# One pair of output products moved ahead of the transposes in each attention chunk, and one gate product at the Fourier head tied behind another

## The chip, the core and the metric

The kernel runs on one core of a Trainium2 chip. The core's engines run side by side, each through its own queue in order: TensorE (PE in the profile, its weight loads as PEld), VectorE (DVE), ScalarE (ACT), GpSimd (POOL) and SyncE (SP), which here issues DMAs only. The metric is the device time of one execution in microseconds, and of several runs the median.

## The reference

Two layers are applied to 2048 prompt tokens and, on its own, to 512 sample tokens, all of width 1024 in float32:

```python
def attention_layer(x, g, w_in, w_out, sink, rel_bias):
    h = rmsnorm(x, g);  z = h @ w_in            # q, k, v and gate
    o = banded_gqa_with_sink(q, k, v, rel_bias, sink)   # |i-j| <= 128, 16 heads of 64, 4 kv heads
    return x + (o * jax.nn.silu(gate)) @ w_out
def fourier_layer(x, g, w_gate, w_out):
    h = rmsnorm(x, g)
    f = jnp.fft.fftn(hg, axes=(1, 3), norm="ortho").real   # hg: h in 4 groups of 256 channels
    return x + (f * jax.nn.silu(h @ w_gate)) @ w_out
```

A last rmsnorm follows. Attention is computed in blocks of 128 queries, each with its own block of keys and the two beside it, a bias from a table and a sink per head.

## The kernel before, in words

Every product of float32 matrices is made of three matmuls on a high and a low part of each factor (high by high, high by low, low by high), summed in PSUM.

**Attention phase.** The tokens are taken in five chunks of 512 (`CHUNKS`): the sample's first, then the prompt's four; here they are the first to the fifth or last chunk. After its projections of k and v, a chunk runs a loop of 19 steps (`for n in range(19)`, about line 1188). The 8 head pairs by 2 pairs of query blocks make 16 rounds, and step n works on up to four rounds at once. The order within a step is written out in the table `PERIOD` (`FIRST` for the first chunk). The entries that matter here, in the table's order, with the engine:

- S1, S2 (PE): the scores of two query blocks, each six matmuls into `spt`, two half arrays side by side (`scores`, line 661).
- b1b, b1a, b2a, b2b (DVE): bias and row minimum of the scores of one block and one head (`biased`, line 680). e1b, e1a and so on (ACT): their exponentials.
- m2a, m1b, m1a: the division by the row's sum, on DVE (line 703) or ACT (701).
- T0, T1 (PE): 12 transposes of the divided weights of a block (line 720) into `tp`; hi0, hi1 (ACT, 733) and lo0, lo1 (DVE, 737) take their high and low parts to `pts`.
- AV1, AV2 (PE, 780): weights by values; add (DVE, 810), mul (POOL): the gated output.
- A and B (PE): the slots for products that don't depend on this step's attention.

On PE, and for these operations on DVE and ACT, the written order is kept by a chain of ordering ties (`chain`, `seq`, `pe`). What stands in A and B comes from `fills(n)`. Each entry is a pair of half products: one runs on the upper 64 rows of the array, the other on the lower 64, at the same time, three matmuls each (`beside`, line 512). Up to step 14 they are projections, at steps 15 and 16 products of the chunk's output projection (weights `wo`, input `uT`). At step 15 `t3` lies in the PSUM bank `pj_72` and `t2` in `pj_73`. When a product goes on in the other row half of its bank, `swapped` (line 528) first puts an empty PE instruction there that waits until the last matmul of the first half is finished:

```python
if before:
    wait = pe(PE.nop())
    for ins in before:
        tc.add_manual_dep(wait.ins, ins.ins.name, DONE, reason="other rows of a bank")
```

`beside` calls it once, for all the pairs that it is given, before the first of them. At step 15 the transposes T1 belong to the last head pair; those of its two other blocks follow at step 16, as that step's T0 and T1.

**Fourier phase.** It works through ten pairs of 128-token tiles (the first: tiles 16 and 17 of the sample). Here the order on each engine is set by the scheduler of the framework, from the order of the code and the dependencies. `gates(pr, hooks)` computes the gates of a pair in four sums W, Z, X and again W, with the weights B11, T1, T2, B22, T3, N4 and, for X, four tiles `b21` (b in the profile) that SP loads one by one: each step of X asks for the next tile (`more`, line 1463). `prod(ps, left, right, ks, first, ...)` issues a product, and takes as a last argument an instruction behind which it is ordered. In the same stretch PE computes the transforms `z17`, `z19` and so on (line 1425) into double banks that are shared with the transposes `trb`; ACT and DVE take these away (lines 1364, 1371, 1377, 1378). x1_4 and x1_0 are the inputs of a later pair; SP loads them (line 1321) when their places are free.

Of the kernel before, what the change touches and what calls it, by code (L numbers as in the profile page):

```python
# [55 lines left out]
def encoder(  # L56
# [147 lines left out]
    def attention_phase():  # L204

        with ExitStack() as es:
# [307 lines left out]
            def beside(*pairs):  # L514

                swapped([(unit[0].last, h) for pair in pairs for h, unit in enumerate(pair) if unit is not None])
                for upper, lower in pairs:
                    both = []
                    for h, unit in enumerate((upper, lower)):
                        if unit is not None:  # L520
                            both.append((unit[0], h) + unit[0].parts(unit[1], slice(64 * h, 64 * h + 64)))
                    for i, j in ((0, 0), (0, 1), (1, 0)):
                        for out, h, a, b in both:
                            out.last[h] = pe(PE.matmul(out.ps, a[i], b[j], **out.flags()))  # L524
# [567 lines left out]
            for c in range(len(CHUNKS)):  # L1092
# [41 lines left out]
                four = range(4)  # L1134

                def fills(n):

                    t0, t1, t2, t3 = op_tiles
                    if n < 15:
                        x, y = (o + (t3,))[n + 1 : n + 3]  # L1140
                        return [((x, 4 + k), (y, k)) for k in four], [((y, k), (x, 4 + k)) for k in four]
                    if n == 15:
                        return [((t3, 4 + k), (t2, k)) for k in range(2)], [((t2, k), (t3, 4 + k)) for k in range(2)]
                    if n == 16:
                        return [((t2, 2 + k), (t1, k)) for k in four], [((t1, k), (t2, 2 + k)) for k in four]
                    return [], []
# [43 lines left out]
                for n in range(19):  # L1190
                    if c == 0:
                        if n + 5 < len(fetches):
                            fetches[n + 5]()
                    if n % 2 == 0 and n < 14:
                        at[n // 2 + 1].start(None if c else last_fetch[0])
                    if c and n < 16:
                        loads[n + 4]()
                    chain.setdefault(PE, None)
                    first, second = fills(n)
                    if n == 16:  # L1200
                        beside(*first[:1])
                        first = first[1:]
                    order = [a for a in (PERIOD if c else FIRST) if n < 15 or a[0] not in ("hi0", "lo0")]
                    if n == 1 and c:
                        order.sort(key=lambda a: a[0] == "qL")
                    if n >= 15:
                        for name, behind in (("hi0", ("T0",)), ("lo0", ("m2a", "m2b"))):
                            at_ = max(i for i, a in enumerate(order) if a[0] in behind)
                            order.insert(at_ + 1, (name, 1))
                    for name, back in order:  # L1210
                        m = n - back
                        if name == "A":
                            beside(*first)
                        elif name == "B":
                            beside(*second)
                        elif name == "qH":
                            if c and 0 <= m < 15:
                                high_q.append(evacs[m + 1])
                            if high_q:
                                low_q.append(high_q.pop()())  # L1220
                        elif name == "sc":
                            if 0 <= m < 15:
                                high_q.append(evacs[m + 1]())
                        elif name == "W":
                            for i in (n + 4,) if n < 15 else (19,) if n == 16 else ():
                                low_w.append(highs[i]())
                        elif name == "WL":
                            if low_w:
                                low_w.pop()()
                        elif name == "side":  # L1230
                            side(n)
                        elif name == "qL":
                            if low_q:
                                low_q.pop()()
                            if k_lows:
                                k_lows.pop()()
                        elif name[:5] == "extra":
                            if n < 17:
                                for i in range(4 * n + 2 * int(name[5]), 4 * n + 2 * int(name[5]) + 2):
                                    extra(i)  # L1240
                        elif 0 <= m < 16 and (name, m) != ("AV2", 15):
                            at[m // 2].ops[2 * (m % 2)][name]()
                    if n % 2 and n < 15:
                        at[n // 2 + 1].sinks()
# [11 lines left out]
    def fourier_phase(tail):  # L1256
        with ExitStack() as es:
# [189 lines left out]
            def prod(out, a, b, ks, first, behind=None):  # L1447

                for k in ks:
                    cs = slice(k * P, (k + 1) * P)  # L1450
                    end = matmul3(
                        out, (a[0][:, cs], a[1][:, cs]), b[k], first and k == 0, k == 3, not first, None if k > ks[0] else behind
                    )
                return end

            b21 = []
# [9 lines left out]
            def gates(pr, hooks):  # L1466

                n, A, S = pr.n, pr.A, pr.S
                W = psum2.tile([P, 512], F32, tag="acc", name=f"W{n}")
                Z = psum2.tile([P, 512], F32, tag="acc", name=f"Z{n}")  # L1470
                X = psum2.tile([P, 512], F32, tag="acc", name=f"X{n}")

                def x_step(k):
                    prod(X, A[0, 1], b21[4 * n : 4 * n + 4], (k,), True)
                    more()

                def silu(c, i, half):
                    th = main.tile([P, 512], F32, tag="xr", bufs=3, name=f"gt{pr.ts[i]}_{half}")
                    ACT.activation(th, c, AF.Silu)
                    t = pr.ts[i]  # L1480
                    dst, t0 = (s2d[0], t) if t < SEQ // P else (s2d[1], t - SEQ // P)
                    POOL.dma_start(dst[t0 * P : (t0 + 1) * P, half * 512 : half * 512 + 512], th)

                def hook(i):
                    for h in hooks.get(i, ()):
                        h()

                four = range(4)
                c = xtile([P, 2, 512], F32, f"c{n}")
                c11, c22 = c[:, 0], c[:, 1]  # L1490
                prod(W, A[0, 0], wg["B11"], four, True)
                ACT.copy(c11, W)
                hook(0)
                x_step(0)
                if pr is pairs[-1]:

                    more()
                    more()
                prod(Z, S[1], wg["T1"], four, True)
                ACT.copy(c22, Z)  # L1500
                hook(1)
                prod(W, S[2], wg["T2"], four, False)
                c12 = fp.tile([P, 512], F32, tag="c12", bufs=1, name=f"c12_{n}")
                ACT.copy(c12, W)
                hook(2)
                x_step(1)
                prod(Z, S[4], wg["B22"], four, False)
                DVE.tensor_tensor(c12, c12, Z, ALU.add)
                silu(c12, 0, 1)
                hook(3)  # L1510
                x_step(2)
                prod(W, S[3], wg["T3"], four, False)
                last_c[0] = DVE.tensor_tensor(c22, c22, W, ALU.add)
                silu(c22, 1, 1)
                hook(4)
                x_step(3)
                DVE.tensor_tensor(c11, c11, X, ALU.add)
                silu(c11, 0, 0)
                if pr is not pairs[-1]:
                    hook(5)  # L1520
                prod(W, A[1, 1], wg["N4"], (0, 1), False)
                if pr is pairs[-1]:
                    hook(5)
                prod(W, A[1, 1], wg["N4"], (2, 3), False)
                silu(W, 1, 0)
                hook(6)

            wg = {w: [None] * 4 for w in ("B11", "T1", "T2", "B22", "T3", "N4")}
# [40 lines left out]
            for i, s in enumerate(tail):  # L1569
# [7 lines left out]
                if 1 <= i < 9:  # L1577
                    w, k = split_steps[i - 1]
# [523 lines left out]
            A, S = ALU.add, ALU.subtract  # L2102
# [241 lines left out]
```

## Time and profile before

| | before |
|---|---|
| median of the timed runs | 1534.37 us (1533.88, 1534.37, 1534.41) |
| the profiled execution | 1535.48 us, span 1533.7 us |
| granted TensorE clock, mean | 0.998 |
| PE busy | 1520.7 us, 99% of the span |
| DVE, ACT, POOL busy | 73%, 58%, 30% of the span |
| matmuls of `pj` from `wo`, `uT` | 360, mean 390 ns |
| data moved by DMA | 372.71 MB, mean 243 GB/s |

Step 15 of the five chunks lies at about 164.6, 373.0, 577.8, 783.2 and 979.9 us (start of A); the stretch of the Fourier head that the change touches is from 1031 to 1058 us.

In a timeline row stand the start, the duration from the first start to the last end, engine, line, operation, result and inputs, the count, and in brackets the idle time of the engine before it and whose end ended it. Rows of like instructions that follow each other are put together. PE rows of `x12` overlap each other: matmuls on the two row halves run at the same time, and the next starts before the last has ended. A row of waits gives the total, the number and the longest. In a DMA row stand the count, the size and the median time from issue to landing.

### The profile page before, as it was taken

To read this page: it belongs to the slowest core of one execution; us is meant where nothing else is said; L and a number is where in the kernel's file an instruction comes from. 1 tells how busy PE (TensorE), PEld (TensorE's weight loads), DVE (VectorE), ACT (ScalarE), POOL (GpSimd) and SP (SyncE) were. 2 spreads that over 40 slices of the span, in tenths; PEclk is the share of its full clock that TensorE was granted. 3 is DMA by queue.
4 is the path that set the end of the run, shared out by engine and by line. 5 is a ranking of instruction groups with operands and counts; after the bars stand their busy time and mean duration, and the time that the engine had idled before them with its cause. 6 is when DMAs were issued, how large, how long until landed. Compare 5 with 4: busy or idle time off the path is not lost.

```text
span 1533.7 us, 33665 instructions
## 1 busy us (share of the span) xinstructions
PE 1520.7 (99%) x13150; PEld 1351.5 (88%) x13150; DVE 1119.0 (73%) x2431; ACT 890.3 (58%) x1925; POOL 453.1 (30%) x616
## 2 busy tenths in 40 slices
PE   9999999999999999999999999999999999999998
PEld 7999889999899998999988899888888888888886
DVE  5898665777538775468764577667888878888896
ACT  6788534787237883268862577646655654243343
POOL 2576652422414323315124142222212111011100
PEclk9999999999999999999999999999999999999999
DMA  8687687785857766867649666584667679557852
GB/s 310 230 308 250 231 337 279 218 304 172 317 202 239 248 215 239 300 212 228 226 169 380 226 211 234 208 298 165 238 207 250 210 247 413 169 180 277 298 184 91
DMA packets 100730, 372.71 MB, mean 243 GB/s; under 512 B 11235, under 2 KB 22251, under 8 KB 83420
## 3 DMA queue, kind: packets, MB, share of 16 engines
q1 hardware_dynamic: 82716, 297.38, 56.1%
q0 software_dynamic: 16688, 70.04, 11.8%
q10 hardware_dynamic: 1168, 3.15, 0.6%
q8 instruction: 103, 1.69, 0.4%
q14 instruction: 55, 0.45, 0.1%
HBM read 280.06 MB, written 90.47 MB: 242 GB/s over the span
## 4 chain that ended last, share of the span: by engine, by line
PE 88%; DVE 7%; issue 2%; ACT 2%; DMA 1%; POOL 0%; POOLq 0%; DVEq 0%; SPq 0%; ACTq 0%
PE pj L524 27%; PE W L134 6%; PE pj L134 6%; PE av L780 6%; PE tp L134 5%; PE spt L661 5%; PE av L134 5%; PE spt L134 4%; PE tp L720 3%; PE Wo L134 3%; PE Z L134 3%; PE fo L134 2%; PE z L1425 2%; PE Zo L134 2%; PE X L134 2%
## 5 line engine op out<-in xcount | busy, mean ns | idle before, releaser
L524 PE MATMUL pj<-h,wg 64*128 64x512 f32 x1920 | 437.7, 388 | 0.0
L524 PE MATMUL pj<-h,wq 64*128 64x512 f32 x1560 | 379.0, 389 | 0.0
L524 PEld LDWEIGHTS pj<-h,wg 64*128 64x128 f32 x1920 | 332.1, 184 | 13.1
L524 PEld LDWEIGHTS pj<-h,wq 64*128 64x128 f32 x1560 | 284.4, 184 | 9.3 <-DVE q L580 0.2
L680 DVE CUSTOM_DVE_ANT_0 S<-spt,b 128x385 f32<-128x385 f32 (+1 forms) x320 | 164.8, 524 | 80.0 <-PE spt L661 77.2
L688 ACT ACTIVATE S<-S 128x385 f32<-128x385 f32 (+1 forms) x320 | 189.2, 592 | 54.9 <-DVE S L680 35.5
L733 ACT CAST pts<-tp 128x768 fp32r<-128x768 f32 (+1 forms) x160 | 121.3, 758 | 77.3 <-PE av L780 43.0
L737 DVE TENSOR_TENSOR pts<-tp,pts 128x768 fp32r<-128x768 f32 (+1 forms) x160 | 144.0, 900 | 11.9 <-ACT pts L733 11.4
L825 POOL TENSOR_TENSOR uT<-o,uT 128x256 fp32r<-128x256 f32 x75 | 56.4, 752 | 228.2 <-ACT uT L821 227.9
L780 PE MATMUL av<-pts,v 64*128 64x256 f32 (+3 forms) x1680 | 122.2, 262 | 1.0 <-DVE pts L737 0.9
L661 PE MATMUL spt<-kwin,qab 64*128 64x384 f32 (+1 forms) x960 | 121.9, 340 | 0.9 <-DVE S L680 0.7
L134 PE MATMUL fo<-wo,tTu 128*128 128x512 f32 x480 | 113.7, 392 | 0.0
L780 PEld LDWEIGHTS av<-pts,v 64*128 64x128 f32 (+1 forms) x1680 | 108.3, 159 | 3.4 <-DVE pts L737 1.6
L134 PEld LDWEIGHTS fo<-wo,tTu 128*128 128x128 f32 x480 | 88.7, 188 | 18.0
L720 PEld LDWEIGHTS tp<-ident,S 64*128 64x128 f32 x1792 | 90.4, 138 | 8.0 <-DVE pts L737 2.6
L720 PE MATMUL tp<-ident,S 64*128 64x64 f32 x1792 | 93.3, 223 | 0.1
L816 POOL TENSOR_TENSOR o<-o,s 128x256 f32<-128x256 f32 x75 | 55.7, 743 | 109.6 <-DVE o L810 86.2
L661 PEld LDWEIGHTS spt<-kwin,qab 64*128 64x128 f32 x960 | 83.7, 187 | 3.7 <-issue 1.8
L703 DVE TENSOR_SCALAR S<-S 128x384 f32<-128x384 f32 (+1 forms) x192 | 84.4, 468 | 0.3
L279 DVE SCALAR_TENSOR_TENSOR h<-xk,g0s,h 128x512 fp32r<-128x512 f32 x40 | 46.9, 1185 | 51.1 <-ACT h L278 51.1
L524 PE MATMUL pj<-wo,uT 64*128 64x512 f32 x360 | 74.7, 390 | 0.0
L278 ACT ACTIVATE h<-xk,g0s 128x512 fp32r<-128x512 f32 x40 | 28.7, 724 | 77.1 <-POOL xk L274 76.3
(379 smaller groups left out, 3360.2 us busy)
## 6 DMA issues: line engine op xcount, KB each, us to landing
wo<-wsd SPq DMA_DIRECT2D x32, 1024.0 KB, 6.4
wq<-wsd SPq DMA_DIRECT2D x31, 1024.0 KB, 6.6
wg<-wsd SPq DMA_DIRECT2D x31, 1024.0 KB, 5.9
x<-x1d SPq DMA_DIRECT2D x40, 512.0 KB, 4.0
b<-b21d SPq DMA_DIRECT2D x40, 512.0 KB, 5.1
b<-rowd SPq DMA_DIRECT2D x40, 384.0 KB, 4.1
xs<-in_x_dram SPq DMA_DIRECT2D x23, 512.0 KB, 6.1
s2d<-gt POOLq DMA_DIRECT2D x40, 256.0 KB, 4.0
```

The lines of the kernel that those rows point to most:

```text
L134: ins = pe(PE.matmul(out, a[i], b[j], start=start and i + j == 0, stop=stop and i == 1, skip_group_check=more))
L524: out.last[h] = pe(PE.matmul(out.ps, a[i], b[j], **out.flags()))
L661: pe(PE.matmul(spt[j][:, 2 + k0 * P : 2 + k1 * P], res["q"][rows, qp, b * P : (b + 1) * P], kwin[g][rows, kp, b * P + k0 * P : b * P + k1 ...
L680: seq(DVE, DVE.tensor_tensor_reduce(out=s[:, e0:e1], in0=ps[:, 1 + e0 : 1 + e1], in1=st["bias"][:, j, 386 - e1 : 386 - e0][:, ::-1], scale ...
L688: last_exp[0] = seq(ACT, ACT.activation(s[:, e0:e1], s[:, e0:e1], AF.Exp, bias=s[:, 386:387], scale=-1.0, accum_out=s[:, 387:388]))
L703: seq(DVE, DVE.tensor_scalar(s[:, ks], s[:, ks], den, None, ALU.mult))
L720: pe(PE.transpose(ps[h][:, kb, j, :], s[rows, j, 1 + kb * P : 1 + (kb + 1) * P], ident[rows, rows]))
L733: seq(ACT, ACT.copy(hi, ps))
L737: seq(DVE, DVE.tensor_tensor(lo, ps, f32(hi), ALU.subtract))
L780: last[i][h] = pe(PE.matmul(to, v, pt, start=not swap and n == 0, stop=swap and n == len(todo[h]) - 1, skip_group_check=True,))
L816: eng.tensor_tensor(o, o, s, ALU.mult)
L825: low = eng.tensor_tensor(lo, o, f32(hi), ALU.subtract)
```

## The change

At step 15 the slot A gets three pairs instead of two, the third in a `beside` of its own, and B one instead of two. At the first Fourier pair (`n` is 0) the product of W with T2 is ordered behind the end of X's first step.

```diff
                     if n == 15:
-                        return [((t3, 4 + k), (t2, k)) for k in range(2)], [((t2, k), (t3, 4 + k)) for k in range(2)]
+                        return [((t3, 4), (t2, 0)), ((t3, 5), (t2, 1)), ((t2, 0), (t3, 4))], [((t2, 1), (t3, 5))]
...
                         if name == "A":
-                            beside(*first)
+                            beside(*first[:2] if n == 15 else first)
+                            if n == 15:
+                                beside(*first[2:])
...
                 def x_step(k):
-                    prod(X, A[0, 1], b21[4 * n : 4 * n + 4], (k,), True)
+                    x_end = prod(X, A[0, 1], b21[4 * n : 4 * n + 4], (k,), True)
                     more()
+                    return x_end
...
-                x_step(0)
+                x_end = x_step(0)
...
-                prod(W, S[2], wg["T2"], four, False)
+                prod(W, S[2], wg["T2"], four, False, None if n else x_end)
```

On PE in the fourth chunk, the order around step 15's T1 (`tp<-ident,S_7_1`) and S2 (`spt<-kwin`):

```order
 L524 MATMUL pj_72<-wo_0_4_8482,uT_5_7577 128x512
 L524 MATMUL pj_73<-wo_0_0_8188,uT_1_6454 128x512
+L524 MATMUL pj_73<-wo_0_0_8188,uT_0_6407 128x512
+L524 MATMUL pj_72<-wo_0_4_8482,uT_4_7273 128x512
+L524 MATMUL pj_73<-wo_0_0_8188,uT_0_6407 128x512
+L524 MATMUL pj_72<-wo_0_4_8482,uT_4_7273 128x512
+L524 MATMUL pj_73<-wo_0_0_8188,uT_0_6407 128x512
+L524 MATMUL pj_72<-wo_0_4_8482,uT_4_7273 128x512
 L720 MATMUL tp<-ident,S_7_1_8616 128x64 x12
 L661 MATMUL spt_74<-kwin,qab_7_8351 128x384
```

The six matmuls with `uT_0` and `uT_4` stood behind S2's six matmuls, as the first pair of B, and stand ahead of T1 now. The empty instruction with the wait stands ahead of the first of them, in both orders. In the other chunks the rows are the same but for the numbers.

On PE at the Fourier head, before:

```order
L134 MATMUL W_15122<-wB_3_14844,tTb_0_14991 128x512 x3
L134 MATMUL W_15122<-wT_0_14757,S_0_15040 128x512 x2
L134 MATMUL X_15124<-b_0_15053,tTb_1_15000 128x512 x3
L1425 MATMUL z_0_15058<-chan_sb,S_0_14997 128x256 x2
L1425 MATMUL z_0_15058<-chan_sb,tTd_15036 128x256 x2
```

and after the change:

```order
L134 MATMUL W_15122<-wB_3_14844,tTb_0_14991 128x512 x3
L134 MATMUL X_15124<-b_0_15053,tTb_1_15000 128x512 x3
L134 MATMUL Z_15123<-wT_0_14754,S_0_14997 128x512
L1427 MATMUL z_0_15058<-chan_sb,S_0_14997 128x256 x2
L1427 MATMUL z_0_15058<-chan_sb,tTd_15036 128x256 x2
```

The two matmuls of W with T2 (`wT`, `S`) join the ten others of their product behind the transposes of tiles 19 and 18; one matmul of Z moves ahead of the transform z17. Further on, in the 25 us behind this, the scheduler places the last of T3's matmuls and the first of N4's otherwise too.

On SP at the same place, before and after:

```order
L1463 DMA b_2_15142<-b21d_133 128x1024
L1463 DMA b_3_15233<-b21d_134 128x1024
L1463 DMA b_4_15259<-b21d_131 128x1024
L1463 DMA b_5_15283<-b21d_132 128x1024
L1321 DMA x_4_15329<-x1d 128x1024
L1321 DMA x_0_15331<-x1d 128x1024
```

```order
L1323 DMA x_4_15329<-x1d 128x1024
L1465 DMA b_2_15142<-b21d_133 128x1024
L1465 DMA b_3_15233<-b21d_134 128x1024
L1465 DMA b_4_15259<-b21d_131 128x1024
L1465 DMA b_5_15283<-b21d_132 128x1024
L1323 DMA x_0_15331<-x1d 128x1024
```

The load of x1_4 has moved ahead of four loads of `b21`. It waits, before and now, for DVE's low part of a sum of tile 18 (line 1378, S2_1); b21_2 waits for X's first step.

## The prediction

> **What bounds the kernel now.** I read the page first (busy times, chain), then the list of waits, then timelines of single engines at the places the change touches.
>
> ```profile
> span 1533.7 us, 33665 instructions
> PE 1520.7 (99%) x13150; PEld 1351.5 (88%) x13150; DVE 1119.0 (73%) x2431; ACT 890.3 (58%) x1925; POOL 453.1 (30%) x616
> ...
> PE 88%; DVE 7%; issue 2%; ACT 2%; DMA 1%; POOL 0%; POOLq 0%; DVEq 0%; SPq 0%; ACTq 0%
> ```
>
> TensorE is busy 99% of the span and carries 88% of the chain that ended last. So nothing is gained by hiding work elsewhere; a microsecond is won only where TensorE stands, and lost only where it is made to stand. The chain gives DVE 7%, though: in the attention loop TensorE often runs just behind DVE. In the third chunk, around the place of the edit (loop step 15, where A, T1, S2 and B follow each other), TensorE shows this:
>
> ```profile
> 577.83 1.58 PE L524 MATMUL pj<-wo,uT 64*128 64x512 f32 x12
> 579.39 0.58 PE L720 MATMUL tp<-ident,S 64*128 64x64 f32 x12
> 580.35 0.79 PE L661 MATMUL spt<-kwin,qab 64*128 64x384 f32 x6 [0.37 <-DVE S L680]
> ...
> 580.97 1.77 PE L524 MATMUL pj<-wo,uT 64*128 64x512 f32 x13
> ...
> 583.64 0.53 PE L720 MATMUL tp<-ident,S 64*128 64x64 f32 x12
> ```
>
> The rows are A (two pairs), T1, S2, B (two pairs, and one matmul of the next step) and the next step's T0. Two half products share a step: 13 matmuls make seven starts, and (1.77 - 0.39)/6 = 0.23 us is the step. A pair is three steps, 0.69 us. T1 is six steps; where it does not wait it takes (0.53 - 0.22)/5 x 6 = 0.37 (second chunk, below). A could have handed over at 577.83 + 1.58 - 0.39 + 0.23 = 579.25, so T1 stood 0.14 us and S2 580.35 - 579.39 - 0.37 = 0.59 us. These are the stalls that a third pair ahead of T1 would fill.
>
> ```profile
> 580.35 0.47 PEld L661 LDWEIGHTS spt<-kwin,qab 64*128 64x128 f32 x6 [0.51 <-DVE S L680]
> ```
>
> The weight load waited too and starts in the same 10 ns as the matmul, so a load is exposed behind each such wait. What an exposed load costs is in this row of the Fourier head, a matmul behind a wait that lasts 0.50 us where others last 0.39: 0.11 us.
>
> ```profile
> 1050.74 0.50 PE L134 MATMUL W<-wT,S 128*128 128x512 f32 x1
> ```
> ```profile
> 1050.74 0.19 PEld L134 LDWEIGHTS W<-wT,S 128*128 128x128 f32 x1 [0.28 <-ACT wT L1277]
> ```
>
> The third chunk's stall is therefore 0.14 + 0.59 + 0.11 = 0.84 us. What DVE does meanwhile decides whether filling it helps:
>
> ```profile
> 580.21 0.08 DVE L680 DVE_READ_ACCUMULATOR2_ANT S<- 128x1 f32 x1
> 580.21 0.84 DVE L810 TENSOR_TENSOR o<-av,t 64x256 f32<-64x256 f32 x2
> 581.17 0.56 DVE L680 CUSTOM_DVE_ANT_0 S<-spt,b 128x385 f32<-128x385 f32 x1
> ...
> 581.73 0.54 DVE L680 CUSTOM_DVE_ANT_0 S<-spt,b 128x385 f32<-128x385 f32 x1
> ...
> 582.19 0.95 DVE L737 TENSOR_TENSOR pts<-tp,pts 128x768 fp32r<-128x768 f32 x1
> 583.06 0.41 DVE L703 TENSOR_SCALAR S<-S 128x384 f32<-128x384 f32 x1
> ```
>
> b1a ends at 580.29 and S2 starts 0.06 later. The two adds end at 581.05; b2a then starts at 581.17, when S2 has ended (580.35 + 0.79 = 581.14). From there DVE runs without a gap: b2a, b2b, lo1, m1a, to 583.47. The next T0 needs m1a and starts at 583.64. So **S2's end starts a DVE chain of 2.3 us, and T0 follows it with 0.17 - 0.06 = 0.11 us to spare**. A delay of S2 passes to T0 but for 0.11 us.
>
> **Part 1, the moved pair.** Six matmuls per chunk, 30 in all, move from behind S2 to ahead of T1. No product, copy or DMA is added. The wait for the other row half of the bank stood at the head of B, where T1 and S2 lay between it and the matmul it waits for; now it stands directly behind that matmul. Queued behind it are the third pair, T1, S2 and everything that TensorE does later. No row before shows such a wait of TensorE on itself. Its price b: the matmul before must end instead of being overlapped (0.39 - 0.23 = 0.16), a signal (0.06 by b1a to S2), and an exposed load (0.11): 0.33 us. I take it, since it is put together from rows of the same kind of matmul and wait. Lower bound 0.06, if only the signal stands and the rest overlaps; upper bound 0.41, with the whole load of 0.19 (the row of 1050.74 on PEld) exposed in place of 0.11. The rows of 0.06 and 0.11 are behind waits for other engines and a load of 128 rows, so neither end is excluded.
>
> By the Trainium skill, "TensorE: Matmul & The Clock Gate", Part 3 "The mechanism", TensorE pulls a weight load ahead of matmuls in flight when it is for other rows, so the load would be hidden and b would be 0.22, and the sum below 0.44 us lower. The row of 580.35 disagrees: there the load waits as long as the matmul.
>
> S2 now moves by 0.69 + b minus the stall it fills. Third chunk: 0.69 + 0.33 - 0.84 = 0.18 us later, T0 0.18 - 0.11 = 0.07 later. The fourth chunk's S2 shows the same wait,
>
> ```profile
> 785.76 0.80 PE L661 MATMUL spt<-kwin,qab 64*128 64x384 f32 x6 [0.37 <-DVE S L680]
> ```
>
> so 0.07 again. Second chunk:
>
> ```profile
> 374.36 0.53 PE L720 MATMUL tp<-ident,S 64*128 64x64 f32 x12
> 374.97 0.79 PE L661 MATMUL spt<-kwin,qab 64*128 64x384 f32 x6
> ...
> 378.16 0.58 PE L720 MATMUL tp<-ident,S 64*128 64x64 f32 x11
> ```
> ```profile
> 375.80 0.56 DVE L680 CUSTOM_DVE_ANT_0 S<-spt,b 128x385 f32<-128x385 f32 x1
> ...
> 377.69 0.41 DVE L703 TENSOR_SCALAR S<-S 128x384 f32<-128x384 f32 x1
> ```
>
> Here S2 stood only 374.97 - 374.36 - 0.37 = 0.24, with the load 0.35. S2 comes 0.69 + 0.33 - 0.35 = 0.67 later, b2a starts right at S2's end (375.76), and T0 follows m1a (378.10) by 0.06, so nothing is to spare: **+0.67 us**. This is the largest term. Last chunk:
>
> ```profile
> 980.55 0.93 PE L524 MATMUL pj<-wo,uT 64*128 64x512 f32 x6
> 981.62 0.59 PE L720 MATMUL tp<-ident,S 64*128 64x64 f32 x12
> 982.31 0.79 PE L661 MATMUL spt<-kwin,qab 64*128 64x384 f32 x6
> ...
> 985.61 0.28 PE L720 MATMUL tp<-ident,S 64*128 64x64 f32 x4
> ```
> ```profile
> 985.03 0.34 DVE L703 TENSOR_SCALAR S<-S 128x256 f32<-128x256 f32 x1
> ```
>
> T1 stood 981.62 - (980.55 + 0.93 - 0.16) = 0.30, S2 0.32, load 0.11: 0.73. S2 is 0.29 late, T0 has 985.61 - 985.37 - 0.06 = 0.18 to spare: +0.11. First chunk:
>
> ```profile
> 167.56 0.83 DVE L810 TENSOR_TENSOR o<-av,t 64x256 f32<-64x256 f32 x2
> 168.43 0.56 DVE L680 CUSTOM_DVE_ANT_0 S<-spt,b 128x385 f32<-128x385 f32 x1
> ```
>
> b2a starts behind adds that end at 168.39, more than 1 us after S2: DVE is the limit on its own, a later S2 is covered by it, 0. (If the adds were gone, it would be 0.6 like the second chunk.) The next T0 sets the pace of the last transposes, so I let each delay reach the end. Part 1: 0.67 + 0.07 + 0.07 + 0.11 = **+0.92 us**. With b = 0.06 it is 0.40 (second chunk), then S2 is 0.09 earlier or even, and T0, which has time to spare behind m1a, up to 0.2 earlier in the three others: about -0.2. With b = 0.41, 4 x 0.08 more: +1.24.
>
> **Part 2, the tied product.** At the Fourier head TensorE stood on an ACT copy:
>
> ```profile
> 1033.45 0.58 ACT L1492 COPY c<-W 128x512 f32<-128x512 f32 x1 [0.52 <-PE W L134]
> ...
> 1034.45 0.59 ACT L1364 COPY s<-trb 128x512 f32<-128x512 f32 x1
> ```
> ```profile
> 1034.08 0.73 PE L134 MATMUL W<-wT,S 128*128 128x512 f32 x2 [0.68 <-ACT c L1492]
> ...
> 1035.35 0.40 PE L1425 MATMUL z<-chan_sb,S 128*128 128x256 f32 x2
> ```
>
> The tie takes W's two matmuls out of this place: X's three and one of Z run instead and need no copy. But next is z17, which needs ACT's third copy (ends 1035.04; its bank). Before, it started at 1035.35 with five matmuls done; now at 1035.04 + 0.05 + 0.11 = 1035.20 with four done, and one is 0.23: 0.15 - 0.23, **+0.08 us**. The stall of 0.79 only changes its owner; if ACT's copies came a copy (0.6) earlier, 0.6 would be gained.
>
> Further on, TensorE's order around the last T3 product changes; beside the wait of 0.28 at 1050.74 it has a second one, in the list of waits:
>
> ```profile
> PEld W L134 <- DVE wT L1279: 0.5, 1, 0.5
> ```
>
> Both may vanish, or grow as much, since the product moves against other work by a few matmuls: 0, within 0.5 us either way. On SP's queue the load of x1_4 now stands ahead of four of b21:
>
> ```profile
> 1035.54 9.43 SPq L1463 DMA_DIRECT2D b<-b21d  x4
> 1051.07 4.17 SPq L1321 DMA_DIRECT2D x<-x1d  x2
> ```
> ```profile
> 1053.87 0.86 PE L134 MATMUL X<-b,tTb 128*128 128x512 f32 x3
> ```
> ```profile
> b<-b21d SPq DMA_DIRECT2D x40, 512.0 KB, 5.1
> ```
> ```profile
> DMA to landing us min/median/max: 3.1/3.6/4.1
> ```
>
> x1_4 waits for a DVE result until 1051.07. Before, b21_2 was issued 15 us ahead of that; now it follows at about 1051.4 at the latest (0.32 an issue). X's third step, at 1053.87 before, now has seven matmuls of N4 and one of z ahead of it and two of W behind: (7 - 2) x 0.23 + 0.12 = 1.27 later, 1055.1. The first of the two rows gives the median landing over the span, 5.1 us, the second that of the five such loads between 1035 and 1060, 3.6. By the second b21_2 is there at 1055.0, in time, and I take 0; by the first at 1056.5, **1.4 us** of stall.
>
> The sum is 0.92 + 0.08 + 0 + 0 = **+1.0 us** on a profiled execution of 1535.48 us (span 1533.7). The three timed runs have a median of 1534.37, 1.1 below that execution, so I forecast 1534.4 + 1.0 = **1535.4 us**.
>
> **The rivals.** *The stalls really fill.* If T0 and the last transposes do not follow DVE's chain, the stalls of the second to the last chunk go (0.35 + 0.84 + 0.84 + 0.73 = 2.76) against 4 x 0.33, and the Fourier stall of 0.79 with them: -2.2, so 1532.2 us. For it: 99% busy means a filled stall is a gain. Against it: b2a, lo1, m1a without a gap, and T0 within 0.2 of m1a in every chunk quoted.
>
> *SP's queue (the slower side).* x1_4's wait holds b21_2 back until TensorE is at X's third step: 1.4 us at the price above, 1534.4 + 1.0 + 1.4 = 1536.8, slower by 0.16%. It decides as soon as issue and landing together end after 1055.1, 3.7 us after the latest issue; past 1537.4 it goes if the landing takes 5.7 us. Against it: the five loads of this stretch, 4.1 us at most (0.4 us of stall).
>
> *The change moves places, not time.* With b at 0.06 to 0.15 part 1 is between -0.2 and +0.2: 1534.4 us.
>
> **How the numbers follow.** A measurement of this kernel tells 0.2%, 3.1 us, from no change; 1531.3 to 1537.4 is the same. Chances: forecast 0.50, moves only places 0.20, stalls fill 0.15, SP's queue 0.15. Of the third case a third could lie beyond 1531.3 (T3's waits gone as well, 0.8), so faster 0.05; of the fourth a third beyond 1537.4, and a little of the first, so slower 0.06; same 0.89. The range is 1532.6 to 1536.9: it leaves out most of the third case and the tail of the fourth; the forecast's own is 1534.0 to 1536.3.
>
> **What would show it.** Right: in the third to fifth chunks T1 and S2 start without idle time, A is 18 matmuls with one gap of about 0.3 us inside, the DVE chain from b2a to m1a stays closed, and the second chunk's T0 comes 0.67 later counted from A's start. At the Fourier head the idle time stands before z17, released by the copy of L1364 (two lines lower now). Wrong: no gap inside A; T0 coming earlier; idle time before X's third step with a DMA as releaser.

## The result, and the profile after

| | before | after |
|---|---|---|
| median | 1534.41 us (13 runs, 1533.40 to 1536.09) | 1537.36 us (13 runs, 1536.74 to 1538.23) |
| profiled execution | 1535.48 us, span 1533.7 | 1536.97 us, span 1535.0 |

The change makes the kernel slower by 2.95 us, a ratio of 1.0017 (95% interval 1.0010 to 1.0025). That is within the 0.2% called "same", but outside the predicted range: forecast 1535.4 in 1532.6 to 1536.9.

The two spans differ by only 1.3 us, since the profiled execution of before began its first projection about 1.5 us later than that of after. So what a stage costs is read below from the stage itself: the starts of the same matmul, by its place in TensorE's order, in two traces; how much their difference grows from just before the stage to just behind it. For step 15 the stretch runs from ahead of A to T0 and the products behind it, some 7.5 us; in runs of the same order it repeats within 0.04 us in the second to fifth chunk.

| growth of the difference to before, us | second chunk | third | fourth | fifth | Fourier, 1042 to 1066 us |
|---|---|---|---|---|---|
| after | +0.75 | +0.18 | +0.18 | +0.26 | +2.08 |
| forecast | +0.67 | +0.07 | +0.07 | +0.11 | 0 |

The Fourier head itself (1028 to 1042 us) grew by 0.07, and of the +2.08 some 0.45 came back by 1082 us. The first chunk's step 15 grew by nothing, as forecast. From there to the end of the program the difference grows by 2.94 us in all, as much as the medians differ.

**Step 15 after.** TensorE in the second chunk; the columns are those of the rows in the prediction:

```profile
370.91 2.58 PE L524 MATMUL pj<-wo,uT 64*128 64x512 f32 x18
373.32 0.54 PE L720 MATMUL tp<-ident,S 64*128 64x64 f32 x12
373.67 0.78 PE L661 MATMUL spt<-kwin,qab 64*128 64x384 f32 x6
...
376.85 0.59 PE L720 MATMUL tp<-ident,S 64*128 64x64 f32 x12
```
```profile
372.52 0.53 PEld L524 LDWEIGHTS pj<-wo,uT 64*128 64x128 f32 x6 [0.50 <-PE pj L524]
```

Eighteen matmuls make nine starts: 8 x 0.23 + 0.39 = 2.23 us without a stop. They took 2.58, so the wait inside A costs 0.35 us. The row of the weight load shows it: idle 0.50, ended by TensorE's own matmul. T1 and S2 no longer stand, as wanted. From A to T0 it is 376.85 - 370.91 = 5.94 us; before it was 378.16 - 372.97 = 5.19:

```profile
372.97 1.55 PE L524 MATMUL pj<-wo,uT 64*128 64x512 f32 x12
```

VectorE in the second and in the third chunk, the row of b2a:

```profile
374.48 0.56 DVE L680 CUSTOM_DVE_ANT_0 S<-spt,b 128x385 f32<-128x385 f32 x1 [0.87 <-PE spt L661]
```
```profile
580.08 0.56 DVE L680 CUSTOM_DVE_ANT_0 S<-spt,b 128x385 f32<-128x385 f32 x1 [0.39 <-PE spt L661]
```

VectorE now waits 0.87 and 0.39 us for S2 where it waited 0.13 and 0.12 (375.80 after adds that ended at 375.67, the row below from before; 581.17 after 581.05). That is the stall of TensorE, handed on.

```profile
374.83 0.84 DVE L810 TENSOR_TENSOR o<-av,t 64x256 f32<-64x256 f32 x2
```

**The Fourier head after.** TensorE's weight loads with idle time before them, from 1034 to 1062 us:

```profile
1034.26 0.30 PEld L1427 LDWEIGHTS z<-chan_sb,S 128*128 128x128 f32 x2 [1.20 <-ACT s L1366]
...
1050.23 0.19 PEld L134 LDWEIGHTS W<-wT,S 128*128 128x128 f32 x1 [0.75 <-ACT wT L1279]
1051.34 0.30 PEld L1427 LDWEIGHTS z<-chan_sb,S 128*128 128x128 f32 x2 [0.82 <-issue]
...
1055.09 0.53 PEld L134 LDWEIGHTS X<-b,tTb 128*128 128x128 f32 x3 [0.18 <-DMA b<-b21d]
1057.09 0.53 PEld L134 LDWEIGHTS X<-b,tTb 128*128 128x128 f32 x3 [0.55 <-DMA b<-b21d]
1061.58 1.50 PEld L134 LDWEIGHTS z<-chan_sb,tTb 128*128 128x128 f32 x12 [1.15 <-ACT z L1400]
```

The same place before, for the last of these rows:

```profile
1060.49 1.49 PEld L134 LDWEIGHTS z<-chan_sb,tTb 128*128 128x128 f32 x12 [0.28 <-ACT z L1398]
```

Ahead of z17 the stall stands as forecast. At T3's last product and at z19 TensorE's loads stand 0.75 + 0.82 us; before, they stood 0.28 + 0.51, both at products of T3. X's third and fourth step wait for their loads, and the second half of z18 waits 1.15 for ScalarE instead of 0.28. Why ScalarE is late, and what the queue did, stands in these rows: SP's issues, the median landing times of the loads and stores from 1047 to 1062 us, then ScalarE's last gate, after and before.

```profile
1050.06 0.32 SPq L1323 DMA_DIRECT2D x<-x1d  x1
1050.47 2.03 SPq L1465 DMA_DIRECT2D b<-b21d  x4
1054.09 0.32 SPq L1323 DMA_DIRECT2D x<-x1d  x1
```
```profile
b<-b21d SPq DMA_DIRECT2D x5, 512.0 KB, 7.8
x<-x1d SPq DMA_DIRECT2D x2, 512.0 KB, 6.3
s2d<-gt POOLq DMA_DIRECT2D x4, 256.0 KB, 5.9
```
```profile
1060.43 0.60 ACT L1482 ACTIVATE gt<-W 128x512 f32<-128x512 f32 x1 [0.98 <-DMA s2d<-gt]
```
```profile
1058.38 0.60 ACT L1479 ACTIVATE gt<-W 128x512 f32<-128x512 f32 x1 [0.52 <-PE W L134]
```

Four loads that had been spread over 9.4 us go out within 2.0, between two more: 3 MB in 4.3 us. The loads of `b21` (these four and one issued at 1058) land after a median of 7.8 us instead of 3.6. The stores of the gates, issued by GpSimd, are slowed too (5.9; 3.4 before). The four gates share three places (`bufs=3`), so ScalarE's last gate needs the place that the first gate's store reads. That store went out at 1052.42 and landed 7.9 us later, at 1060.3; the gate starts at 1060.43, idle 0.98 us before it, released by the store. Before, the first gate's store landed after 4.2 us. The row of all four stores before, then the first store alone, after and before:

```profile
s2d<-gt POOLq DMA_DIRECT2D x4, 256.0 KB, 3.4
```
```profile
s2d<-gt POOLq DMA_DIRECT2D x1, 256.0 KB, 7.9
```
```profile
s2d<-gt POOLq DMA_DIRECT2D x1, 256.0 KB, 4.2
```

### The profile page after: what moved, and what is told of

It reads as the page before. It is cut to its first block, busy times and chain, and to the rows that moved or that the text cites. A ratio compares the mean times of both kernels' runs of the same rounds, so it can differ in the third digit from the quotient of the medians.

```text
span 1535.0 us, 33664 instructions
## 1 busy us (share of the span) xinstructions
PE 1520.4 (99%) x13150; PEld 1330.0 (87%) x13150; DVE 1118.4 (73%) x2431; ACT 891.2 (58%) x1925; POOL 454.4 (30%) x616
## 3 DMA queue, kind: packets, MB, share of 16 engines
q8 instruction: 103, 1.69, 0.4%
## 4 chain that ended last, share of the span: by engine, by line
PE 88%; DVE 7%; issue 2%; ACT 2%; DMA 1%; POOL 0%; POOLq 0%; ACTq 0%; DVEq 0%; SPq 0%
PE pj L524 27%; PE W L134 6%; PE pj L134 6%; PE av L780 5%; PE tp L134 5%; PE spt L661 5%; PE av L134 5%; PE spt L134 4%; PE tp L720 4%; PE Wo L134 3%; PE Z L134 3%; PE fo L134 2%; PE z L1427 2%; PE Zo L134 2%; PE X L134 1%
```

## The experiments

Each stands beside the kernel before, run on the same chip. Ratios carry their 95% interval. "In the trace" means the growth of the difference, as defined above, in the second to the fifth chunk or over the stretch that is named, from one profiled execution of each kernel. In the diffs, `...` stands for lines left out.

**p1_alone: the moved pair without the tie.**

```diff
                     if n == 15:
-                        return [((t3, 4 + k), (t2, k)) for k in range(2)], [((t2, k), (t3, 4 + k)) for k in range(2)]
+                        return [((t3, 4), (t2, 0)), ((t3, 5), (t2, 1)), ((t2, 0), (t3, 4))], [((t2, 1), (t3, 5))]
...
                         if name == "A":
-                            beside(*first)
+                            beside(*first[:2] if n == 15 else first)
+                            if n == 15:
+                                beside(*first[2:])
```

> The moved pair alone, without the tie at the Fourier head. Theory (each chunk pays the wait of 0.33 us inside A and DVE's chain passes it on): the sum of the steps that the changed kernel's trace shows at step 15, about +0.8 in the second chunk and +0.1 to 0.2 in the third, fourth and fifth, +1.3 us in all, 1535.7 us against 1534.4. Rival (the stalls are really filled and what the change cost came from the Fourier head alone): 1534.4 us or less.

1536.04 us beside 1534.58: ratio 1.0010 (1.0001 to 1.0019), +1.46 us. In the trace: +0.75, +0.20, +0.18, +0.26, in all +1.40, and nothing at the Fourier head. The moved pair alone costs what its own step shows.

**p2_alone: the tie without the moved pair.**

```diff
...
-                x_step(0)
+                x_end = x_step(0)
...
-                prod(W, S[2], wg["T2"], four, False)
+                prod(W, S[2], wg["T2"], four, False, None if n else x_end)
```

> The tie at the Fourier head alone, step 15 as before. Theory (the head itself costs 0.1, the new order behind it 0.8 and the bunched loads 1.1): +1.9 us, 1536.3 us. Rival (the tie is neutral, as the forecast had it): +0.1, 1534.5 us.

1536.38 us: ratio 1.0013 (1.0003 to 1.0022), +1.80 us. In the trace +0.07 to 1042 us and +1.91 to 1066, of which 0.22 came back. The two parts add up to 3.26 us, where both together gave 2.95.

**p1_no2: the moved pair in the third to fifth chunk only.**

```diff
                     if n == 15:
-                        return [((t3, 4 + k), (t2, k)) for k in range(2)], [((t2, k), (t3, 4 + k)) for k in range(2)]
+                        return ([((t3, 4), (t2, 0)), ((t3, 5), (t2, 1)), ((t2, 0), (t3, 4))], [((t2, 1), (t3, 5))]) if c > 1 else ([((t3, 4 + k), (t2, k)) for k in range(2)], [((t2, k), (t3, 4 + k)) for k in range(2)])
...
```

> The moved pair alone, and only in the third, fourth and fifth chunks; the first two as before. Theory (the second chunk, whose stall ahead of S2 is shorter than the third pair, carries half of the loss): 1.40 - 0.75 = +0.65 us of 1.40, 1535.1 us beside 1534.4 to 1534.6 before; the three chunks keep their +0.2, +0.2 and +0.26. Rival (what is lost in one chunk is made up for in the next): the loss of the moved pair alone, +1.4, or none.

1534.91 us beside 1534.70: ratio 1.0003 (0.9994 to 1.0012). The trace has +0.01 in the second chunk and +0.18, +0.20, +0.26 in the others, +0.66 in all and no recovery between them. The time is in line with +0.65 but cannot tell it from nothing; the trace can.

**p1_mid: the third pair between T1 and S2.**

```diff
...
                     for name, back in order:
...
+                        if name == "S2" and n == 15:
+                            beside(*first[2:])
                         if name == "A":
-                            beside(*first)
+                            beside(*first[:2] if n == 15 else first)
```

> The moved pair alone, but the third pair stands between T1 and S2 instead of ahead of T1, so that T1 covers the wait for the other row half. Theory (the price is the wait of 0.33 us, as far as DVE's chain has no time to spare): S2 0.34 us late in the second chunk, not late in the third and fourth, 0.25 late in the last with 0.18 to spare: +0.4 us, 1534.8 us, and no idle weight load ahead of the third pair. Rival (the six matmuls ahead of S2 cost it, wherever they stand): +1.3 us, 1535.7 us.

1535.35 us beside 1534.58: ratio 1.0005 (0.9996 to 1.0014), +0.77. In the trace +0.41, +0.03, +0.02, +0.28: half of p1_alone's loss, but more than the +0.4 in all that the theory had. The time alone can't tell it from no change. No weight load of the third pair waits any more. S2, which now follows products instead of transposes, takes 0.69 us where it takes 0.78 behind T1 in the kernel after. The third pair follows T1 now and takes 0.94 us where 2 x 0.23 + 0.39 = 0.85 would do, so a load stays exposed behind T1:

```profile
372.87 0.94 PE L524 MATMUL pj<-wo,uT 64*128 64x512 f32 x6
373.65 0.69 PE L661 MATMUL spt<-kwin,qab 64*128 64x384 f32 x6
```

What is gone is the wait inside A. Counted from A's start, S2 ends 0.35 us earlier than in p1_alone in the second chunk (after 3.19 us instead of 3.54), the whole wait. In the third and fourth it ends 0.17 and 0.16 earlier, since T1 comes 0.14 us later there than in the second; in the fifth it does not end earlier (+0.02), since T1 comes 0.38 later: the stall ahead of T1, which the pair had filled from inside A, is back. So the wait inside A is what the third and fourth chunk pay, and in the second what is left is the pair itself, ahead of an S2 that had stood too short a time to cover it.

**s2_first: the reverse remedy.** Two and two pairs as before, but S2 ahead of T1 and VectorE's b1b and b1a ahead of lo0.

```diff
+                    if n == 15 and c:
+                        low = order.index(("lo0", 1))
+                        last = max(order.index((a, 0)) for a in ("b1b", "b1a"))
+                        if low < last:
+                            order.insert(last + 1, ("lo0", 1))
+                            order.pop(low)
+                        order.remove(("S2", 0))
+                        order.insert(order.index(("T1", 1)), ("S2", 0))
```

> Pairs as before (two in A, two in B); at step 15 of the second to the fifth chunk DVE's b1b and b1a stand ahead of lo0 and S2 ahead of T1, so that S2's end no longer waits behind lo0. Theory (DVE's chain from S2's end to m1a sets T0): b2a up to 0.3 us earlier in the third and fourth chunk, T0 0.1 to 0.3 earlier in each, 1533.8 us. Rival (TensorE's own work sets T0): no change, 1534.4; if T1, now last, makes hi1 and lo1 late: slower by up to 0.5.

1533.39 us beside 1534.70: ratio 0.9993 (0.9984 to 1.0002), -1.3. In the trace -0.19, -0.46, -0.50, -0.49: 1.63 us, more than expected. This profiled execution (1535.10 us) is slower than the median: 0.72 us was given back where TensorE waited for the last residuals, ahead of the Fourier head, and 0.94 behind 1284 us. VectorE runs on to b2a without a wait:

```profile
577.53 0.56 DVE L680 CUSTOM_DVE_ANT_0 S<-spt,b 128x385 f32<-128x385 f32 x1
...
578.49 0.95 DVE L737 TENSOR_TENSOR pts<-tp,pts 128x768 fp32r<-128x768 f32 x1
579.36 0.84 DVE L810 TENSOR_TENSOR o<-av,t 64x256 f32<-64x256 f32 x2
580.23 0.56 DVE L680 CUSTOM_DVE_ANT_0 S<-spt,b 128x385 f32<-128x385 f32 x1
```

**s2_three: s2_first with the change's three pairs in A.**

> The order of s2_first (S2 ahead of T1, DVE's b1b and b1a ahead of lo0, in the second to fifth chunk) with the moved pair on top: three pairs in A, one in B, in all chunks, wait for the other row half included. Theory (the moved pair costs because S2's end starts DVE's chain, and here DVE comes to b2a only 0.8 us after S2's end): the pair's 0.69 + 0.33 us hide behind DVE's lo0 and adds in the third to fifth chunk, local change against before near s2_first's -0.5 per chunk (-0.3 to -0.6) instead of +0.2; second chunk, with less cover, -0.2 to +0.3. Sum 1533.3 to 1534.3. Rival (the wait inside A is lost wherever S2 stands): 1.4 us above s2_first, 1534.8.

1535.81 us beside 1534.44: ratio 1.0008 (0.9999 to 1.0017). In the trace +0.69, +0.12, +0.12, +0.22: the theory's -0.3 to -0.6 was wrong, and the rival nearer, though the sum is 2.8 us above s2_first's and not its 1.4. The row of b2a, in the third chunk, says why:

```profile
580.18 0.56 DVE L680 CUSTOM_DVE_ANT_0 S<-spt,b 128x385 f32<-128x385 f32 x1 [0.65 <-PE tp L720]
```

Not S2 released it but T1: b2a writes the scores of block 2 to one of two places, and T1 still reads that place. Whichever of T1, S2 and VectorE's own work ends last starts the chain, so turning the two round does not shield it from a pair ahead of both.

**s2_mid: s2_first with the third pair between S2 and T1.**

> The order of s2_first with the third pair between S2 and T1 (S2 covers the wait for the other row half) and one pair in B, in the second to fifth chunk. Theory: TensorE's wait of 0.4 ahead of T1 is filled, but the next T0 is then held by m1a on DVE, whose work is the same: within 0.2 us of s2_first, 1533.4 us. Rival (TensorE's stall was the limit): another 0.4 in each of three chunks, 1532.3 us.

1534.72 us: ratio 1.0002 (0.9993 to 1.0011). In the trace +0.38, -0.19, -0.20, -0.13, some 0.3 to 0.6 worse than s2_first in each chunk. Both expectations missed; T1 is later by the pair, and b2a is released by it (idle 0.33 us in the third chunk), as in s2_three.

**s2_three_sep and s2_first_sep: another place for block 2's scores.** This takes away what makes b2a wait for T1.

```diff
-                        st[b] = ap.tile([P, 2, 388], F32, tag="S", bufs=2, ...)
+                        st[b] = ap.tile([P, 2, 388], F32, tag="bias" if (p, b) == (7, 2) and c else "S", bufs=2, ...)
...
```

For it the bias tables are made as wide as the scores (388 instead of 386). First s2_three_sep:

> s2_three, but the scores of the last head pair's block 2 (which b2a writes) get the place of a bias table that is free by then, instead of the place that T1 still reads. The trace of s2_three shows b2a released by T1, 0.65 us after DVE was through with the adds, and not by S2. Theory (DVE's chain starts with b2a, and b2a follows whichever of T1, S2 and DVE's own work ends last): b2a comes 0.38 earlier, 0.03 after S2's end; local change against before -0.26 in the third and fourth chunk (was +0.12), -0.16 in the fifth (was +0.22), +0.31 in the second (was +0.69): -0.4 in all where s2_three had +1.15. Rival (TensorE's wait inside A and its work set T0, b2a is incidental): as s2_three, +1.15.

1534.99 us beside 1534.29: ratio 1.0004 (0.9995 to 1.0013). In the trace +0.51, -0.05, -0.06, +0.03, in all +0.44 where s2_three had +1.15.

```profile
580.03 0.56 DVE L680 CUSTOM_DVE_ANT_0 S<-spt,b 128x385 f32<-128x385 f32 x1 [0.26 <-PE spt L661]
...
580.59 0.54 DVE L680 CUSTOM_DVE_ANT_0 S<-spt,b 128x385 f32<-128x385 f32 x1
...
581.24 0.96 DVE L737 TENSOR_TENSOR pts<-tp,pts 128x768 fp32r<-128x768 f32 x1
```

b2a is released by S2 now and waits 0.26 us in place of 0.65. This shows that b2a's start sets a good part of T0: 0.71 us of the trace's growth went by a place in memory, with TensorE's order at step 15 unchanged. The 0.71 is less than the 1.5 expected, because b2b ends at 581.13 (580.59 + 0.54) and lo1 starts at 581.24. That lo1 waits there for T1 by way of ScalarE's hi1 is argued from the order; no run takes it apart. The times of the two kernels, +0.70 and +1.37, go the same way but don't tell them apart.

Then s2_first_sep:

> s2_first with the same other place for block 2's scores. There b2a already starts 0.03 us after DVE's adds. Theory: nothing to gain, the four chunks as with s2_first, -0.2 and three times -0.45 to -0.5, 1533.4 us. Rival (T1 held b2a there too): 0.1 to 0.3 more in each.

1533.31 us beside 1534.29: ratio 0.9992 (0.9983 to 1.0001). In the trace -0.18, -0.49, -0.50, -0.47, as s2_first, and here nothing was given back at the Fourier head: TensorE is still 2.7 us ahead at the last products, 1.5 of them from the start of the program. This and s2_first are the only kernels here with medians below before's; both intervals still touch 1.

**p2_sp_back: the tie with SP's old order.** The load of x1_4 is tied behind b21_5.

```diff
                     load = queue.dma_start(self.x[i], x1d[t * P : (t + 1) * P, :])
+                    if t == 4:
+                        after(load, last_b21[0])
...
```

> The tie alone, with the load of x1_4 tied behind b21_5 on SP, which is SP's order before. Theory (SP's order is what bunches the loads): the waits before X's third and fourth step and most of ScalarE's delay before z18 vanish, 1.1 of 1.9 us goes, +0.8 us, 1535.2 us; the waits at T3's last product and at z19's second half stay. Rival (TensorE's and ScalarE's own new order costs it, loads are incidental): 1536.3 us, as with the tie alone.

1535.11 us beside 1534.58: ratio 1.0005 (0.9996 to 1.0014). The weight loads with idle time before them, from 1049 to 1062 us:

```profile
1049.10 0.19 PEld L134 LDWEIGHTS W<-wT,S 128*128 128x128 f32 x1 [0.78 <-ACT wT L1277]
1050.21 0.30 PEld L1427 LDWEIGHTS z<-chan_sb,S 128*128 128x128 f32 x2 [0.82 <-issue]
...
1058.87 1.49 PEld L134 LDWEIGHTS z<-chan_sb,tTb 128*128 128x128 f32 x12 [0.27 <-ACT z L1400]
```

The waits for b21 are gone, z18 waits 0.27 as before the change, and the two waits of TensorE's new order (0.78, 0.82) stay. From 1042 us to the products at 1065 us the difference to before grows by 0.74 us instead of 1.9. Behind it comes a new wait of 1.35 us at the next transposes, most of it won back by 1108 us (+0.96 from 1042 us), and another 1.14 us is lost from 1284 to 1296 us, where s2_first loses 0.66 and p2_alone nothing. So the time, +0.53, bears out the theory only with its interval; the trace up to 1065 us does so plainly.

**held_loads: bunched loads without the change.** In the kernel before, b21_2 to b21_5 wait on SP for VectorE's part of tile 18.

```diff
-                    SP.dma_start(f32(t), f32(b21d[k % 4]))
+                    load = SP.dma_start(f32(t), f32(b21d[k % 4]))
+                    if held[0] is not None and k < 6:
+                        tc.add_manual_dep(load.ins, held[0].ins.name, DONE, reason="held")
...
                 hook(2)
+                if not n:
+                    held[0] = last_part[0]
+                    more()
...
```

> Nothing of the change; the kernel before with b21_2 to b21_5 held on SP until DVE's part of tile 18 that releases x1_4 is done, so that four loads and then x1_4 go out within some 4 us, as with the tie but with x1_4 last. Theory (bunched loads alone cost time): X's steps wait 0 to 0.5 us, and ScalarE's last gate waits for a store that lands late, so that z18 stands 0.5 to 0.9 longer; +0.5 to +1.2 us, 1535.0 to 1535.8. Rival (bunching is harmless without TensorE's new order): within 0.2 us of before.

1536.86 us beside 1534.70: ratio 1.0021 (1.0012 to 1.0030), +2.16, more than the theory's upper end. From 1042 to 1066 us the trace's difference to before grows by 1.69 us. X's steps wait for nothing; ScalarE's last gate and z18 do:

```profile
1058.36 0.60 ACT L1482 ACTIVATE gt<-W 128x512 f32<-128x512 f32 x1 [2.01 <-DMA s2d<-gt]
```
```profile
1059.51 1.49 PEld L134 LDWEIGHTS z<-chan_sb,tTb 128*128 128x128 f32 x12 [1.95 <-ACT z L1398]
```

With six loads of 512 KB within 4.2 us the stores land after a median of 6.8 us (3.4 before). Bunching costs here about what the tie costs (+2.16 and +1.80, with intervals that overlap). Not the loads alone differ: the scheduler also puts five of N4's matmuls ahead of X's third step. But ScalarE's gate is released by a store.

**head_fill: more work ahead of z17.**

```diff
...
-                prod(Z, S[1], wg["T1"], four, True)
...
+                z_end = prod(Z, S[1], wg["T1"], (0, 1), True)
+                pr.z_odd_even(1, z_end)
+                prod(Z, S[1], wg["T1"], (2, 3), True)
...
```

These lines are for the first pair; the call for z17 moves here from its old place, and W's product is tied as in the change.

> Step 15 as before; at the Fourier head W's T2 product behind X's first step as in the change, and z17 behind half of Z's product, so that nine matmuls stand ahead of z17 instead of four. Theory (the stall of 0.78 with its exposed load of 0.11 is worth its length if enough work stands ahead): -0.9 us at the head; the transposes of tiles 19 and 18 stand later by the scheduler's choice, which may cost up to 1 us behind it: 1533.5 to 1534.6 us. Rival (the stall only moves on, as with the tie): 1534.5 us or more, with a new wait of 0.8 within 10 us.

1535.71 us beside 1534.70: ratio 1.0008 (0.9999 to 1.0017). The stall at z17 is gone, and the two waits at T3's last product have grown from 0.28 and 0.51 to:

```profile
1045.52 0.19 PEld L134 LDWEIGHTS W<-wT,S 128*128 128x128 f32 x1 [0.86 <-ACT wT L1277]
1047.35 0.30 PEld L134 LDWEIGHTS W<-wT,S 128*128 128x128 f32 x2 [1.64 <-DVE wT L1279]
```

0.86 + 1.64 - 0.79 = 1.71 us, twice what was filled. In the trace the difference to before grows by 1.87 us from 1028 to 1066 us, and 0.92 of it comes back by 1108. The time alone can't tell it from no change, but the trace bears out the rival: TensorE came sooner to products whose factors ScalarE and VectorE had not made yet.

## Why the prediction was wrong

**Held.** That the stalls of step 15 would be filled and come back through VectorE (p1_alone, and the idle time of b2a). The price of the wait inside A: 0.33 us forecast, 0.35 measured. The second chunk as the largest term: +0.67 against +0.75; the first chunk's 0 (b2a starts 0.98 us behind S2's end there, where the prediction read more than 1; it is cover enough). At the Fourier head +0.08 forecast, +0.07 measured, the stall moving to z17. The time to spare ahead of T0: counted from A's start, S2 comes 0.25, 0.25 and 0.37 us later than before in the third to fifth chunk and T0 0.14, 0.13 and 0.18, so 0.11 to 0.19 was taken up where 0.11 and 0.18 were forecast. The likeliest sign, slower, and within 0.2%.

By the Trainium skill, "TensorE: Matmul & The Clock Gate", Part 3 "The mechanism", a weight load for other rows is pulled ahead of matmuls in flight, which gave 0.22 us for the wait. The trace does not show this across a wait: after the third pair's first matmul the next step starts 0.33 us later, not 0.23, so the load was not hidden.

**Mis-sized: the exposed load in the stall that is filled.** The step "the third chunk's stall is therefore 0.14 + 0.59 + 0.11" counted S2's exposed load as part of what the third pair recovers, 0.11 us in each of four chunks. It is not recovered: S2 takes 0.79 us with a wait ahead of it and still 0.78 without one (373.67, after), but 0.69 behind products (p1_mid, where the third pair pays the load behind T1 in its place). That T1's transposes, some 0.06 us a step, are too short to hide a load of 0.18 is the likely reason; no run changes their length. Counted from A's start, S2 comes 0.76, 0.25, 0.25 and 0.37 us later, where 0.67, 0.18, 0.18 and 0.29 were forecast: 0.07 to 0.09 more in each. With 0.11 more, the forecast's 0.67, 0.07, 0.07, 0.11 become 0.78, 0.18, 0.18, 0.22, in all 1.36, against 1.40 measured in p1_alone. Part of that agreement is luck: the T0s themselves come 1.20 us later, and the last 0.2 us is added behind them and not taken apart.

**Failed: "0" for the order at T3 and "I take 0" for SP's queue.** The tie, which brings both, costs 1.8 us in time (p2_alone). The two waits at T3 (one of them now at z19) grew by 0.75 + 0.82 - 0.79 = 0.78 us, beyond the 0.5 that was allowed either way. For the queue the issue time was well guessed: b21_2 goes out at 1050.5 in a trace that runs 0.8 us ahead of before's here, so at 1051.3 by before's time, with at most 1051.4 forecast. The landing was not. The prediction took 3.6 us, the median of loads that had gone out at most two at a time, for loads that would go out four at a time with two others: the second of the four, b21_3, took 6.1. The rival that named the queue priced the median of the whole span, 5.1 us, and looked only at X. X waited 0.73 us, and a DMA as releaser ahead of X's third step was the sign of being wrong that the prediction had named. The larger part, 0.87 us more at z18, came by a path that neither named: late stores, a gate's place not free, ScalarE late. p2_sp_back takes both away at once by SP's order and leaves 0.74 us of the tie's 1.91, held_loads makes the second alone.

**The rivals.** "The stalls really fill" (1532.2) fell with p1_alone. "SP's queue" (1536.8) had the right place and a price in the right range by the wrong path: it put 1.4 us on X alone, where SP's order is worth 1.91 - 0.74 = 1.17 in the trace, and X waits only 0.59 in p2_alone, z18 0.95 - 0.27 = 0.68 more than in p2_sp_back; that the sizes agree is luck. "Moves places, not time" fell with the 0.35 us inside A. Its low end for part 1, -0.2, doesn't follow from the prediction's own rows either: with S2 0.09 us earlier, T0 can't come 0.2 earlier.

What stays open: how the 2.08 us of the Fourier stretch with both parts divide between TensorE's order and the loads to the last tenth, because the waits follow on each other, and because each tie lets the scheduler order later work otherwise.

## What to carry to other kernels

A stall that a moved product fills is a gain only if the engine that starts from the stalled instruction's end is not itself the limit: follow it to the next instruction that waits for it, and add the price of any wait that moves with the product. When an edit changes the order of a DMA queue, price the loads at the landing of a bunch and list every buffer that any transfer of that moment sets free, stores too. Where the engine behind TensorE is late, its own order (s2_first, -1.6 us in the trace, though its time is not clear of no change) or a second place for its result (s2_three_sep, 0.7 us of s2_three's loss) did what more filler could not.

## What the runs showed of the hardware

- A wait of TensorE for its own last matmul, with the other row half next, costs 0.35 us beside a step of 0.23.
- The first weight load behind transposes of 64 columns is not hidden: S2 takes 0.78 us there and 0.69 behind products of 512 columns; the third pair takes 0.94 there (p1_mid), where its steps without a stop come to 0.85.
- Loads issued by SP slow stores that GpSimd issued: with 3 MB in 4.3 us, stores of 256 KB landed after a median of 5.9 us instead of 3.4 (6.8 in held_loads), loads of 512 KB after 7.8 instead of 3.6. The Trainium skill, "DMA: Bandwidth & Descriptors", section "Issuing engines are not separate DMA queues", says that transfers of all issuing engines run on the same 16 DMA engines and interleave; these rows agree.
